# A hybrid decoder layer on one core: the order of the high and low products inside a weight half

## The chip, the core and the metric

The kernel runs on one core of a Trainium2 chip. The metric is the device time of one execution in microseconds. A core has five engines, each with its own instruction queue: TensorE (PE; its weight loads are listed apart as PEld), VectorE (DVE), ScalarE (ACT), GpSimd (POOL) and SyncE (SP), which issues the DMAs here. An engine works off its queue in order and waits on semaphores for what other engines make.

## The reference, cut to what matters

One layer of a decoder trunk over 2048 prompt tokens and 8 x 8 sample tokens, model width 1024, all in fp32: a norm with modulation, the input projection `w_in`, four recurrent mixers (RWKV-7, GLA, gated delta rule, SSD) side by side, the output projection `w_out` with a gated residual, a second norm, and a squared-ReLU MLP with 4096 hidden columns, then a final norm.

```python
h = rmsnorm(x, p['norm1_w']) * (1 + sc1) + sh1
u = jnp.einsum('btd,de->bte', h, p['w_in'])
...
y = jnp.concatenate([y_a, y_b, y_c, y_d], -1) @ p['w_out']
x = x + gt1 * y
h = rmsnorm(x, p['norm2_w']) * (1 + sc2) + sh2
f = jnp.square(jax.nn.relu(h @ p['w_up'])) @ p['w_down']
x = x + gt2 * f
```

The recurrences make the mixers a long chain of small operations; the four projections are the dense work.

## The kernel before

**Three products for one.** TensorE multiplies in fp32r, which holds fewer bits than fp32. So each fp32 operand is split into a high part (its rounding to fp32r) and a low part (the rest), and of the four products three are added up in PSUM: high weight x high activation (line 118), high weight x low activation (line 119), low weight x high activation (line 120). These three lines are nearly all of TensorE's work.

**Weights.** `wload` brings 128 output columns x 1024 inputs of a weight matrix in two halves of 512 (four blocks of 128 inputs each). Per half: a DMA into `wr` (line 100), a cast on ScalarE into the high part `wh` (line 101), and a subtraction `wr - wh` into the low part `wl` (line 103), on VectorE and GpSimd by turns. The rings hold 4 raw, 3 high and 3 low halves, so the cast of a half waits until the high part three halves earlier has had its last reader.

**Products.** `mm3` runs over the four blocks of a half and issues the three products of a block one behind the other. `project` does this for both halves, and in each half for one or two token tiles of 320 to 360 tokens, each with a PSUM bank of its own. A one-tile half is 12 products, a two-tile half 24. The banks are a ring of three (`DPS`).

**Stages.** `stage_A` computes the input projection in four passes over the tokens: one tile, two tiles, two tiles, one tile (`A_PASSES`); ScalarE evacuates each bank into `uo` (line 302), which goes to DRAM. The mixers work on blocks of 256 tokens as soon as their columns are there; their matmuls write `psm`. Beside them go the output projection `F_out` (its transposes are line 338) and the MLP of the first two token blocks, one tile each: `F_up` makes four hidden tiles `f` (ReLU and square on ScalarE, the high part cast there, the low part by VectorE in line 506), and `F_down` multiplies these four with two halves of `w_down` per load, one output tile per half, and adds the result into `acc` on VectorE (line 315). The last 1400 tokens come after the mixers: `quad` computes the up projection by a scheme with seven products of half-size blocks for eight (`forms_w` makes its weight combinations, split in lines 363 and 367), first for one pair of token tiles (from about 2400 us), then for two, and `F_down2` the down projection. All of these call `mm3`.

**Order.** Each lane of the kernel has its priorities: two lanes of mixers go before the dense work, which fills what they leave. The order of every engine's queue is worked out when the kernel is built, by a planner that goes by estimated durations (`schedule_with_timeline_sim=True`, line 2403) and takes what its estimate finds ready; on the chip it is then fixed. So products of mixers stand in the midst of dense groups, and the groups of several PSUM banks can be interleaved.

Of the kernel before, what the change touches and what calls it, by code (L numbers as in the profile page):

```python
# [36 lines left out]
class Dense:  # L37
# [71 lines left out]
        self.tc.add_manual_dep(dma.ins, self.w_dma, mybir.DependencyInfo(mybir.DependencyClass.NoSync, mybir.DependencyReason.SCHED_ONLY),  # L109
                               reason="weights first")  # L110

    def mm3(self, ps, w, ks, first=True, last=True, **kw):

        nc = self.nc
        whi, wlo = w
        for i, (xh, xl) in enumerate(ks):
            lh, ll = whi[:, i * 128 : i * 128 + 128], wlo[:, i * 128 : i * 128 + 128]
            nc.tensor.matmul(ps, lhsT=lh, rhs=xh, start=first and i == 0, stop=False, **kw)  # L118
            nc.tensor.matmul(ps, lhsT=lh, rhs=xl, start=False, stop=False, **kw)  # L119
            nc.tensor.matmul(ps, lhsT=ll, rhs=xh, start=False, stop=last and i == len(ks) - 1, **kw)  # L120

    def project(self, src, xs, tag="d"):

        w = self.wload(src)
        out = [self.psum(tag)[:, :n] for n, _, _ in xs]
        for h in range(2):
            for ps, (n, hi, lo) in zip(out, xs):
                self.mm3(ps, w[h], [(hi[:, k], lo[:, k]) for k in range(4 * h, 4 * h + 4)], h == 0, h == 1)
        return out


# [2275 lines left out]
```

## Time and profile before

| | |
|---|---|
| median of three runs | 3448.45 us (3440.43 to 3454.96) |
| profiled execution | 3452.71 us, span of its instructions 3450.4 us |
| mean granted TensorE clock | 0.953 |
| TensorE busy, products | 3223.8 us (93%), 22902 |
| VectorE / ScalarE / GpSimd busy | 2277.8 / 1474.2 / 1399.2 us |

In the profile's rows PE is a matmul and PEld the load of its weights, which overlaps the matmul before; each product has one of each. `psd<-a,wh` reads: into a PSUM tile `psd`, from the activations `a` and the high weights `wh`; `wl` is the low part, `f` a hidden tile, `sl` a tile of the last stage, `psm` a bank of the mixers. L120 is line 120. A releaser behind `<-` is the instruction whose end let the waiting one go.

### The profile page before, as it was taken

Reading aid. Unit: us, or ns where it says so; the run is one execution under the profiler, and the core shown is the slowest. Engines: PE = TensorE matmul, PEld = TensorE weight load, DVE = VectorE, ACT = ScalarE, POOL = GpSimd, SP = SyncE. Lnnn points to the kernel's source line nnn. Section 1 sums busy time; section 2 is a strip of 40 time slices with the busy share of each in tenths; the row PEclk is TensorE's granted clock in tenths of the full one; section 3 lists DMA queues with packets and bytes.
Section 4 is the critical chain, followed back from the end, with each engine's and each line's share of the span. In section 5 each row is a group of like instructions: output and inputs, shape, how many; then the busy total and the mean of one; then the engine's idle time right before and its main releaser. Section 6 shows DMA issues by size and latency. Waiting matters only on the chain. (4 is left out here: it accounts for less than half of the span.)

```text
span 3450.4 us, 62464 instructions
## 1 busy us (share of the span) xinstructions
PE 3223.8 (93%) x22902; PEld 2947.5 (85%) x22902; DVE 2277.8 (66%) x4728; ACT 1474.2 (43%) x3054; POOL 1399.2 (41%) x1290
## 2 busy tenths in 40 slices
PE   8999999899998989999989988888879999999997
PEld 4779898897997978888868978767879999999997
DVE  3437665866668778889879768768384355445446
ACT  3443433434354454464554454444455566111113
POOL 2333334624335346345446336236275365212112
PEclk9999999999999999999989989978899999999998
DMA  9863344423244565343443333444444455322213
GB/s 301 260 189 114 88 102 134 138 81 108 93 116 124 149 140 137 99 121 103 129 135 121 101 105 96 130 138 152 155 122 125 139 162 173 113 68 99 69 34 122
DMA packets 350394, 438.61 MB, mean 127 GB/s; under 512 B 100626, under 2 KB 228394, under 8 KB 350088
## 3 DMA queue, kind: packets, MB, share of 16 engines
q1 hardware_dynamic: 350088, 434.63, 41.5%
q8 instruction: 180, 2.95, 0.4%
q14 instruction: 126, 1.03, 0.1%
HBM read 346.75 MB, written 87.74 MB: 126 GB/s over the span
## 5 line engine op out<-in xcount | busy, mean ns | idle before, releaser
L103 POOL TENSOR_TENSOR wl<-wr,wh 128x512 fp32r<-128x512 f32 x344 | 477.3, 1389 | 1073.4 <-ACT wh L101 938.6
L120 PE MATMUL psd<-a,wl 128*128 128x360 f32 (+3 forms) x2368 | 798.1, 338 | 25.8 <-DVE wl L103 21.3
L101 ACT CAST wh<-wr 128x512 fp32r<-128x512 f32 x688 | 421.9, 617 | 900.3 <-PE psd L119 418.9
L118 PE MATMUL psd<-a,wh 128*128 128x360 f32 (+3 forms) x2368 | 794.4, 337 | 7.0 <-ACT a L254 3.3
L119 PE MATMUL psd<-a,wh 128*128 128x360 f32 (+3 forms) x2368 | 792.1, 335 | 6.3 <-DVE a L258 2.8
L120 PEld LDWEIGHTS psd<-a,wl 128*128 128x128 f32 x2368 | 456.3, 193 | 67.3 <-DVE wl L103 27.1
L118 PEld LDWEIGHTS psd<-a,wh 128*128 128x128 f32 x2368 | 457.4, 193 | 32.6 <-issue 11.0
L119 PEld LDWEIGHTS psd<-a,wh 128*128 128x128 f32 x2368 | 457.6, 193 | 20.9 <-issue 8.2
L103 DVE TENSOR_TENSOR wl<-wr,wh 128x512 fp32r<-128x512 f32 x344 | 286.5, 833 | 161.6 <-ACT wh L101 145.9
L118 PE MATMUL psd<-sl,wh 128*128 128x350 f32 x992 | 325.8, 329 | 20.9 <-DVE r L484 5.8
L118 PE MATMUL pse<-sl,wh 128*128 128x350 f32 x992 | 325.2, 328 | 7.8 <-DVE s L478 6.0
L120 PE MATMUL pse<-sl,wl 128*128 128x350 f32 x992 | 323.8, 328 | 8.1 <-POOL wl L103 3.8
L119 PE MATMUL psd<-sl,wh 128*128 128x350 f32 x992 | 323.7, 326 | 0.0
L119 PE MATMUL pse<-sl,wh 128*128 128x350 f32 x992 | 322.7, 325 | 0.0
L120 PE MATMUL psd<-sl,wl 128*128 128x350 f32 x992 | 321.6, 326 | 0.3 <-DVE wl L367 0.2
L118 PEld LDWEIGHTS psd<-sl,wh 128*128 128x128 f32 x992 | 189.4, 191 | 23.5 <-issue 6.9
L118 PEld LDWEIGHTS pse<-sl,wh 128*128 128x128 f32 x992 | 189.6, 191 | 9.3 <-ACT wh L363 6.6
L120 PEld LDWEIGHTS pse<-sl,wl 128*128 128x128 f32 x992 | 189.0, 191 | 9.9 <-POOL wl L103 4.0
L118 PE MATMUL psd<-f,wh 128*128 128x352 f32 (+1 forms) x512 | 174.6, 349 | 21.0 <-DVE acc L315 9.1
L120 PEld LDWEIGHTS psd<-sl,wl 128*128 128x128 f32 x992 | 189.5, 191 | 1.2 <-DVE wl L367 0.9
L119 PEld LDWEIGHTS psd<-sl,wh 128*128 128x128 f32 x992 | 190.4, 192 | 0.0
L119 PEld LDWEIGHTS pse<-sl,wh 128*128 128x128 f32 x992 | 189.9, 191 | 0.0
(632 smaller groups left out, 6304.1 us busy)
## 6 DMA issues: line engine op xcount, KB each, us to landing
wr<-w_in SPq DMA_DIRECT2D x256, 256.0 KB
wr<-w_up SPq DMA_DIRECT2D x212, 256.0 KB
wr<-w_down SPq DMA_DIRECT2D x208, 256.0 KB
ada<-ada_w SPq DMA_DIRECT2D x96, 256.0 KB
wr<-w_out SPq DMA_DIRECT2D x96, 256.0 KB
u<-uo SPq DMA_DIRECT2D x128, 180.0 KB
fd<-r SPq DMA_DIRECT2D x128, 175.0 KB
sl<-fd SPq DMA_DIRECT2D x32, 700.0 KB
```

The source lines that it names most:

```text
L101: nc.scalar.copy(hi, raw)
L103: self.lo_eng[self.lo_i % len(self.lo_eng)].tensor_tensor(out=lo, in0=raw, in1=hi.bitcast(F32), op=ALU.subtract)
L118: nc.tensor.matmul(ps, lhsT=lh, rhs=xh, start=first and i == 0, stop=False, **kw)
L119: nc.tensor.matmul(ps, lhsT=lh, rhs=xl, start=False, stop=False, **kw)
L120: nc.tensor.matmul(ps, lhsT=ll, rhs=xh, start=False, stop=last and i == len(ks) - 1, **kw)
```

## The change

`mm3` no longer goes block by block through all three products. It has two parts: first the two products with the high weights for all four blocks, then the product with the low weights for all four. A new argument `half` says whether both parts are issued ("hl") or one of them. `project` issues a first weight half in two goes, the high part of all token tiles and then the low part of all of them; in the second half each token tile has its high and low products together. `F_down`, `F_down2` and `quad` call `mm3` as before and get the new order inside each half. With one tile both halves are then 8 high and 4 low products; with two tiles the first half is 8 + 8 high and 4 + 4 low, the second 8 high, 4 low, 8 high, 4 low.

```diff
-    def mm3(self, ps, w, ks, first=True, last=True, **kw):
+    def mm3(self, ps, w, ks, first=True, last=True, half="hl", **kw):
 
         nc = self.nc
         whi, wlo = w
-        for i, (xh, xl) in enumerate(ks):
-            lh, ll = whi[:, i * 128 : i * 128 + 128], wlo[:, i * 128 : i * 128 + 128]
-            nc.tensor.matmul(ps, lhsT=lh, rhs=xh, start=first and i == 0, stop=False, **kw)
-            nc.tensor.matmul(ps, lhsT=lh, rhs=xl, start=False, stop=False, **kw)
-            nc.tensor.matmul(ps, lhsT=ll, rhs=xh, start=False, stop=last and i == len(ks) - 1, **kw)
+        cols = lambda t, i: t[:, i * 128 : i * 128 + 128]
+        if "h" in half:
+            for i, (xh, xl) in enumerate(ks):
+                nc.tensor.matmul(ps, lhsT=cols(whi, i), rhs=xh, start=first and i == 0, stop=False, **kw)
+                nc.tensor.matmul(ps, lhsT=cols(whi, i), rhs=xl, start=False, stop=False, **kw)
+        if "l" in half:
+            for i, (xh, _) in enumerate(ks):
+                nc.tensor.matmul(ps, lhsT=cols(wlo, i), rhs=xh, start=False, stop=last and i == len(ks) - 1, **kw)
 
     def project(self, src, xs, tag="d"):
 
         w = self.wload(src)
         out = [self.psum(tag)[:, :n] for n, _, _ in xs]
         for h in range(2):
-            for ps, (n, hi, lo) in zip(out, xs):
-                self.mm3(ps, w[h], [(hi[:, k], lo[:, k]) for k in range(4 * h, 4 * h + 4)], h == 0, h == 1)
+            ks = range(4 * h, 4 * h + 4)
+            for half in ("hl",) if h else ("h", "l"):
+                for ps, (n, hi, lo) in zip(out, xs):
+                    self.mm3(ps, w[h], [(hi[:, k], lo[:, k]) for k in ks], h == 0, h == 1, half)
         return out
```

## The prediction

> **What bounds the kernel now.** I read the page's totals first, then the busy time by stage, then TensorE's own list of waits, and at last single places in the timeline.
>
> ```profile
> span 3450.4 us, 62464 instructions
> ...
> PE 3223.8 (93%) x22902; PEld 2947.5 (85%) x22902; DVE 2277.8 (66%) x4728; ACT 1474.2 (43%) x3054; POOL 1399.2 (41%) x1290
> ```
>
> TensorE is busy for 3223.8 of 3450.4 us, so 226.6 us of idle time is what a change of order alone could win directly. The busy time in stretches (columns: stretch, its length, then busy time and count for PE, PEld, DVE, ACT and POOL, granted clock, DMA share, GB/s) shows where that idle time lies:
>
> ```profile
> 195.00:1060.00 865.00, 836.61 (x6572) 751.36 (x6571) 570.56 (x1407) 363.61 (x822) 337.00 (x365) 0.97 0.40 114
> 1060.00:1345.00 285.00, 254.42 (x1947) 227.51 (x1945) 227.76 (x498) 133.46 (x293) 141.16 (x137) 0.93 0.58 143
> 1345.00:2400.00 1055.00, 956.70 (x7404) 863.27 (x7405) 859.28 (x1889) 508.56 (x1059) 472.51 (x440) 0.92 0.39 119
> 2400.00:2600.00 200.00, 162.66 (x914) 156.36 (x913) 128.70 (x170) 95.33 (x193) 105.73 (x80) 0.91 0.43 132
> 2600.00:3400.00 800.00, 798.61 (x4962) 798.06 (x4961) 378.99 (x528) 277.72 (x481) 270.52 (x170) 1.00 0.33 107
> ```
>
> From 2600 to 3400 us TensorE never rests: 800 / 4962 gives 0.161 us from one product to the next, and the order of products cannot help there. From 195 to 1060 us (the two passes with two token tiles) it idles 28 us. From 1060 to 2600 us, where every projection has one token tile and VectorE is over 80% busy up to 2400, it idles 30.6 + 98.3 + 37.3 = 166 us. TensorE's waits (us in total, times, longest) name the part that the change speaks to, and three others that I use below:
>
> ```profile
> PE psd L120 <- DVE wl L103: 30.2, 22, 3.7
> PE psd L120 <- POOL wl L103: 6.0, 6, 2.0
> PE pse L120 <- POOL wl L103: 3.8, 1, 3.8
> PE pse L120 <- DVE wl L367: 2.6, 2, 2.4
> PE pse L120 <- POOL wl L367: 1.7, 1, 1.7
> PE psd L119 <- DVE f L506: 1.6, 2, 1.4
> PE psm L1077 <- DVE dq L1043: 4.5, 1, 4.5
> PE psd L118 <- ACT uo L302: 0.3, 1, 0.3
> ```
>
> The first five rows are the low product (line 120) standing for the low part of a weight half: 32 waits, 44.3 us. In the order of time they begin at 1066 us, all in one-tile stretches, and between 195 and 1060 us there is none. One of them, TensorE and then VectorE at the same moment (start, length, instruction):
>
> ```profile
> 1319.52 0.32 PE L120 MATMUL psd<-a,wl 128*128 128x352 f32 x1
> 1322.12 0.43 PE L120 MATMUL psd<-a,wl 128*128 128x352 f32 x1 [2.28 <-DVE wl L103]
> 1322.39 0.32 PE L118 MATMUL psd<-a,wh 128*128 128x352 f32 x1
> ```
> ```profile
> 1319.61 0.68 DVE L1366 TENSOR_TENSOR t<-t,t 128x512 f32<-128x512 f32 x1
> 1320.21 0.83 DVE L844 COPY t<-gla 128x512 f32<-128x512 f32 x1
> 1320.97 1.10 DVE L103 TENSOR_TENSOR wl<-wr,wh 128x512 fp32r<-128x512 f32 x1
> ```
>
> VectorE is not idle: it works off mixer instructions, and the subtraction that makes the low part stands behind them in its queue. The high part of that half is there, and six more products with it stand in TensorE's queue behind the waiting one.
>
> **The change part by part.** *What stays.* 22902 products and as many weight loads; no DMA, cast, subtraction, PSUM evacuation or buffer is added or removed, so the 3223.8 us of work stay and only idle time and clock can move.
>
> *The low product goes later.* In a one-tile half the first low product is the third of 12 now and the ninth after, 6 x 0.161 = 0.97 us more for the subtraction. At most 32 x 0.97 = 31 us come back. In the timeline 29 of these waits are over 0.3 us, the shortest and the longest being
>
> ```profile
> 1345.28 0.43 PE L120 MATMUL psd<-f,wl 128*128 128x352 f32 x1 [0.34 <-DVE wl L103]
> 2506.40 0.43 PE L120 MATMUL pse<-sl,wl 128*128 128x350 f32 x1 [3.75 <-POOL wl L103]
> ```
>
> 19 of the 29 are longer than 0.97 us and give back 0.97 each (18.4 us), the other 10 all they have (5.5 us): 24 us. Five follow another within 9 us, and there the late VectorE is met again at the next half, so I take 5 off: **-19 us**. Bounds: 0, if each gap only moves to the next wait (VectorE is 81% busy there), and -31.
>
> *The high part comes free earlier.* Its last reader is the eighth product of 12 now in place of the eleventh, 3 x 0.161 = 0.48 us earlier, so ScalarE's next cast can begin earlier. Where I looked (rows above) the subtraction waited for VectorE and not for the cast: I take 0. Bounds 0 and 32 x 0.48 = -15 us.
>
> *The clock.* Idle time costs twice here, because after a stretch with much of it the granted clock halves for one or more stretches of 3.4 us. Four pairs of stretches, before and after such a wait:
>
> ```profile
> 1329.90:1333.30 3.40, 1.27 (x8) 1.28 (x9) 3.40 (x6) 0.50 (x1) 1.52 (x2) 1.00 0.08 16
> 1333.30:1340.10 6.80, 6.80 (x31) 6.80 (x31) 6.19 (x15) 4.40 (x12) 4.09 (x3) 0.50 0.70 206
> 1476.70:1480.10 3.40, 1.74 (x15) 1.26 (x13) 2.91 (x5) 3.40 (x9) 2.19 (x2) 1.00 0.14 38
> 1480.10:1486.90 6.80, 6.80 (x47) 5.85 (x48) 4.03 (x7) 3.15 (x9) 3.31 (x4) 0.50 0.52 159
> 1572.20:1575.60 3.40, 1.34 (x8) 1.34 (x9) 3.40 (x4) 0.71 (x2) 3.40 (x3) 1.00 0.30 98
> 1575.60:1582.40 6.80, 6.80 (x30) 6.19 (x29) 6.80 (x10) 1.80 (x4) 6.70 (x6) 0.50 0.37 116
> 1992.10:1995.50 3.40, 0.80 (x5) 0.81 (x6) 3.37 (x4) 1.11 (x3) 2.00 (x2) 1.00 0.28 64
> 1995.50:2012.60 17.10, 17.10 (x190) 14.57 (x189) 7.44 (x19) 5.40 (x11) 4.84 (x9) 0.50 0.43 119
> ```
>
> Idle time of 2.13, 1.66, 2.06 and 2.60 us in 3.4 stood before them. With 0.97 less the first three fall to 1.2 us and under, below the smallest of the four, the last only to 1.63. I take the first three as saved: 20.4 us at half clock, all busy, are 10 us lost, **-10 us**. Bounds: 0, and (20.4 + 17.1) / 2 = -19 with the fourth.
>
> The Trainium skill ("TensorE: Matmul & The Clock Gate", section "Why this matters for your kernels") asks for no gaps over some 3 us in a row of products, since a whole idle window halves the clock. The trace differs: 1.66 us idle in 3.4 were followed by clock 0.50. By the page's rule none of the three waits above would have cost clock, the term would be 0 and the sum some 10 us smaller.
>
> *What gets worse: the joint between up and down.* F_down's products need four hidden tiles, and the last comes late. The planned order already fills that time by running three PSUM banks up to the last tile:
>
> ```profile
> 2075.51 0.33 PE L118 MATMUL psd<-f,wh 128*128 128x360 f32 x1
> ...
> 2080.91 0.66 PE L118 MATMUL psd<-f,wh 128*128 128x360 f32 x3
> 2082.95 0.43 PE L119 MATMUL psd<-f,wh 128*128 128x360 f32 x1 [1.39 <-DVE f L506]
> ```
>
> Three L118 in a row are three banks arriving at the fourth tile together. Before it they hold 3 x 9 = 27 products; after the change only the high ones of three tiles, 3 x 6 = 18, since the low ones now follow the fourth's high ones. Of the 16 joints 14 go straight over; in six of these the timeline has more than 18 products started before the tile is whole (20, 19, 26, 29, 30, 26), 42 above 18, by 0.161 us **+7 us**. Bounds: 0, where mixer products fill in, and 14 x 9 x 0.161 = +20.
>
> *The two-tile passes.* Both tiles' high products go first, so the second PSUM bank is wanted four products (0.66 us) earlier. The evacuation that frees it takes
>
> ```profile
> L302 ACT COPY uo<-psd x192: 408/452/484, 48.6 to 1309.8; 128x360 f32<-128x360 f32 x128, 128x320 f32<-128x320 f32 x32, 128x352 f32<-128x352 f32 x32
> ```
>
> 0.45 us, 20 products (3.2 us) still lie between, and TensorE waited for it 0.3 us in all: +0.5, bounds 0 and 64 x 0.66 = +42, where each copy came just in time, which that row excludes. The low part gets 14 products more there and nobody waits for it: 0. At the start of each of the two passes the second tile's activations are wanted 0.66 us sooner: +1. The products of two-tile quads after 2600 us: 0, TensorE is full there.
>
> *Sum.* -19 - 10 + 7 + 1.5 = -20.5, say -21 us. The profiled execution took 3452.7 us (span 3450.4 and 2.3 around it), 4.3 above the median of the runs, 3448.45; taken off that median it is **3427 us**. The terms' bounds give 3448.5 - 65 = 3383 and 3448.5 + 22 = 3470.
>
> **Rivals.** *The gaps only move (0.30).* The low part is late because VectorE is, and where TensorE no longer stands at line 120 it stands a little later at the next instruction that VectorE owes it. For it: VectorE's 859 of 1055 us. Against: a queue with 19% of slack can catch up within the microsecond given. If a third of the -19 is kept, the stretches stay idle enough for half clock (the page's rule above also gives a clock term of 0, by another road), and the joint costs its 7: 3448.5 - 6 + 7 - 4 (a little of the earlier cast) = 3445.
>
> *The joint decides (0.09), slower.* If in all 14 joints the last tile comes after 18 products and no mixer product is ready, each costs 9 x 0.161 = 1.45 us and, like 1.66 us above, a half-clock stretch of 6.8 us, 3.4 lost: 14 x 4.85 = 68 less 29, 3448.5 + 39 = 3487. For it: the three-bank pattern. Against: 1.6 us of waits for f today. It turns the sign when more than 6 joints (29 / 4.85) pay in full.
>
> *The order is planned anew (0.10), slower.* The order on each engine is worked out when the kernel is built, from estimated durations (line 2403), and longer runs of dense products change what fits between mixer products. One place now costs as follows, when a mixer's serial chain ran with no dense product put beside it:
>
> ```profile
> 1763.40:1797.50 34.10, 18.77 (x115) 15.00 (x114) 26.86 (x48) 19.82 (x43) 15.80 (x15) 0.50 0.34 95
> ```
>
> 15.3 us idle and half of 18.8 lost: 25 us. Two such places more make 3427 + 50 = 3477. One more ends at 3452, no change; the sign turns at one. Against: dense work is the filler and its amount is the same. A luckier plan is as possible and lies in the range's lower end.
>
> **How the numbers follow.** The sum as worked out, with its gain: 0.50, own range 3395 to 3431. With 0.30, 0.09 and 0.10 as above, and 0.01 left over, the predicted time is 3427. What a measurement here tells from no change is about 0.5%, 17 us. Faster by more than that: 0.50; within: 0.31; slower: 0.19. Low end 3390, near the terms' lower bound; high end 3466, which takes in the moving gaps and one unlucky place and leaves out about 0.13 above and 0.06 below.
>
> **What will show it.** Right: the rows of line-120 waits, 44.3 us now, fall under 25; the granted clock, 0.93 and 0.92 in the two stretches from 1060 to 2400, rises by 0.01 or more; PE count stays 22902. Wrong on the joint: waits for f (L506) well over 1.6 us. Gaps moved: the low product's waits fall but waits for acc L315, wh L101 and mixer tiles rise by as much. Replanned: a new stretch like 1763 to 1797. The prediction fails most simply if products with the same rate no longer follow at 0.161 us after 2600 us.

## Result and profile after

| | before | after |
|---|---|---|
| median of the runs beside each other | 3452.03 us (6 runs, 3440.43 to 3454.96) | 3428.98 us (6 runs, 3426.07 to 3431.08) |
| ratio, 95% interval | | 0.9939 [0.9926, 0.9951] |
| span of the profiled execution | 3450.4 us | 3428.5 us |

The changed kernel is 0.6% faster, 21 to 23 us; the prediction was 3427 us and 21 us less. The total came out; the terms behind it only in part, and that the others cancel is luck (the sum is in the part on why). The page's totals of the changed kernel:

```profile
span 3428.5 us, 62450 instructions
...
PE 3196.0 (93%) x22902; PEld 2934.5 (86%) x22902; DVE 2253.6 (66%) x4728; ACT 1475.3 (43%) x3054; POOL 1397.0 (41%) x1290
```

TensorE's idle time did not fall: 3428.5 - 3196.0 = 232.5 us, 226.6 before. All of the gain is in its *busy* time, with the same 22902 products at the same distance. Two things sit in busy time that are no work. Products at half clock count as busy all along. And a product's record lasts 0.32 us where the next one starts after 0.161, so the first 0.16 us of any wait lies under the record of the product before: the wait shown as 2.28 us at 1322.12 was 2.60 from start to start, 2.44 lost. In what follows I therefore add up starts to starts, less 0.161 us (0.147 for 320 columns, 0.165 for 360), and give the rest to half clock or to what the next product waited for.

The stretches of the changed kernel, with the columns as before:

```profile
195.00:1060.00 865.00, 839.95 (x6609) 753.91 (x6608) 583.56 (x1412) 370.06 (x831) 337.74 (x367) 0.97 0.40 115
1060.00:1345.00 285.00, 251.54 (x1924) 226.96 (x1923) 222.32 (x498) 129.75 (x284) 136.20 (x134) 0.90 0.56 141
1345.00:2400.00 1055.00, 941.89 (x7415) 856.57 (x7414) 875.61 (x1900) 513.26 (x1066) 480.45 (x445) 0.92 0.39 119
2400.00:2600.00 200.00, 170.35 (x1008) 167.06 (x1009) 126.18 (x170) 104.58 (x212) 110.76 (x85) 0.93 0.46 145
2600.00:3400.00 800.00, 795.74 (x4934) 794.96 (x4933) 355.49 (x548) 271.15 (x475) 265.56 (x167) 1.00 0.33 110
```

TensorE's waits; the low product is line 123 now, the high ones lines 119 and 120, `f` is made in lines 510 and 511:

```profile
PE psd L119 <- ACT sl L402: 16.6, 1, 16.6
...
PE psd L120 <- DVE f L511: 9.7, 5, 4.8
...
PE psm L1439 <- DVE KB L1416: 8.2, 5, 4.7
...
PE psd L123 <- DVE wl L103: 6.1, 6, 1.9
...
PE pse L123 <- DVE wl L372: 5.4, 2, 4.8
...
PE pse L123 <- POOL wl L103: 2.0, 1, 2.0
...
PE psd L123 <- POOL wl L103: 1.2, 2, 0.7
```

The waits of low products are down from 44.3 us to 16 us (these four rows and two small ones). New on the list are one wait of 16.6 us for `sl`, the activations of the last stage, and more waits for `f` and for mixer tiles.

**Where the time went, by three stretches.** I cut both executions at 1060 us, at the last product of F_down, and at the 1000th product of the last stage.

| stretch | before | after |
|---|---|---|
| 1060 us to the last F_down product | 1340.4 us | 1299.6 us |
| to the 1000th product of the last stage | 223.8 us | 242.5 us |
| to the end | 826.3 us | 826.4 us |

The middle of the kernel gained 41 us and the step into the last stage gave 19 of them back. Within the first stretch (starts to starts, as above):

| 1060 us to the last F_down product, us | before | after |
|---|---|---|
| low product waits for `wl` | 42.0 | 7.6 |
| half clock on dense products | 35.9 | 27.0 |
| PSUM bank not yet free (`acc`, `xp`) | 16.9 | 4.4 |
| waits for `f` | 2.1 | 12.6 |
| mixer products waiting | 55.6 | 79.0 |
| dense products' own time | 757.8 | 748.9 |

Not all of the stretch is in these rows. They add up to 910.3 and 879.5 us; the rest, 430.1 and 420.1 us, mostly the mixers' own products, is 10 us smaller and is not taken apart here. The last row is work that was already done by 1060 us: 9 of the 41 us were won in the passes before, where no low product had waited.

**The step that gives back.** The end of F_down and what follows, first in the kernel before, then in the changed one:

```profile
2400.21 0.32 PE L120 MATMUL psd<-f,wl 128*128 128x360 f32 x1
2400.57 0.40 PE L118 MATMUL psd<-sl,wh 128*128 128x350 f32 x1
```
```profile
2358.90 0.82 PE L123 MATMUL psd<-f,wl 128*128 128x360 f32 x4
2360.50 0.40 PE L119 MATMUL psd<-sl,wh 128*128 128x350 f32 x1 [0.77 <-DVE acc L320]
...
2361.06 0.32 PE L120 MATMUL psd<-sl,wh 128*128 128x350 f32 x1
2377.97 0.66 PE L119 MATMUL psd<-sl,wh 128*128 128x350 f32 x1 [16.59 <-ACT sl L402]
```

Before, the last stage found its activations made and went on at once. After, F_down ends 41 us sooner and TensorE stands before the second block for 16.59 us, because ScalarE and VectorE make these activations no sooner. When each kernel casts the first of them and when it ends F_down shows in these groups (durations, then first and last start), before and then after:

```profile
L397 ACT ACTIVATE sl<-d,mod x24: 573/588/596, 2348.7 to 2572.2; 128x350 fp32r<-128x350 f32 x24
L120 PE MATMUL psd<-f,wl x512: 317/324/667, 1345.3 to 2400.2; 128*128 128x352 f32 x86, 128*128 128x360 f32 x85
```
```profile
L402 ACT ACTIVATE sl<-d,mod x24: 576/587/592, 2355.5 to 2554.9; 128x350 fp32r<-128x350 f32 x24
L123 PE MATMUL psd<-f,wl x512: 318/326/502, 1335.5 to 2359.4; 128*128 128x352 f32 x86, 128*128 128x360 f32 x85
```

I call the start of the first cast of `sl` X and the end of F_down F. Before: X 2349, F 2400. After: X 2356, F 2360.

### The profile page after: what moved, and what is told of

Its sections match the earlier page's. It is cut to its first block, busy times and chain, and to the rows that moved or that the text cites. A ratio compares the mean times of both kernels' runs of the same rounds, so it can differ in the third digit from the quotient of the medians.

```text
span 3428.5 us, 62450 instructions
## 1 busy us (share of the span) xinstructions
PE 3196.0 (93%) x22902; PEld 2934.5 (86%) x22902; DVE 2253.6 (66%) x4728; ACT 1475.3 (43%) x3054; POOL 1397.0 (41%) x1290
## 5 line engine op out<-in xcount | busy, mean ns | idle before, releaser
L123 PE MATMUL psd<-a,wl 128*128 128x360 f32 (+3 forms) x2368 | 504.5, 333 | 6.8 <-DVE wl L103 5.2
L123 PEld LDWEIGHTS psd<-a,wl 128*128 128x128 f32 x2368 | 400.7, 191 | 37.7 <-issue 21.7
L103 DVE TENSOR_TENSOR wl<-wr,wh 128x512 fp32r<-128x512 f32 x344 | 273.3, 795 | 157.8 <-ACT wh L101 122.0
L119 PE MATMUL psd<-sl,wh 128*128 128x350 f32 x992 | 323.7, 328 | 31.5 <-ACT sl L402 16.6
L119 PEld LDWEIGHTS psd<-sl,wh 128*128 128x128 f32 x992 | 190.2, 192 | 33.7 <-ACT sl L402 16.9
L123 PE MATMUL pse<-sl,wl 128*128 128x350 f32 x992 | 200.8, 326 | 7.9 <-DVE wl L372 5.4
L123 PE MATMUL psd<-sl,wl 128*128 128x350 f32 x992 | 200.2, 326 | 0.9 <-DVE wl L372 0.9
L120 PE MATMUL psd<-f,wh 128*128 128x352 f32 (+1 forms) x512 | 171.4, 338 | 9.9 <-DVE f L511 9.7
L877 DVE SCALAR_TENSOR_TENSOR t<-u,cw,t 128x256 f32<-128x256 f32 x288 | 178.5, 659 | 0.9
L119 PE MATMUL psd<-f,wh 128*128 128x352 f32 (+1 forms) x512 | 168.1, 340 | 11.0 <-DVE d L324 4.8
```

Source lines behind the costliest of these rows:

```text
L103: self.lo_eng[self.lo_i % len(self.lo_eng)].tensor_tensor(out=lo, in0=raw, in1=hi.bitcast(F32), op=ALU.subtract)
L119: nc.tensor.matmul(ps, lhsT=cols(whi, i), rhs=xh, start=first and i == 0, stop=False, **kw)
L120: nc.tensor.matmul(ps, lhsT=cols(whi, i), rhs=xl, start=False, stop=False, **kw)
L123: nc.tensor.matmul(ps, lhsT=cols(wlo, i), rhs=xh, start=False, stop=last and i == len(ks) - 1, **kw)
L877: nc.vector.scalar_tensor_tensor(out=y[:, q], in0=uv[:, q, i : i + n], scalar=w(i), in1=y[:, q], op0=ALU.mult, op1=ALU.add)
```

## The experiments

Ratios are to the kernel before on the same chip, with 95% intervals. F and X are of the profiled execution, S is the start of the product that follows the 1000th of the last stage (called the 1000th product below), and wl is the sum of the low products' waits between 1060 us and F (or S for the two kernels marked *).

| kernel | ratio | F | X | S | S - F | S - X | wl |
|---|---|---|---|---|---|---|---|
| before | 1 | 2400.5 | 2348.7 | 2624.2 | 224 | 275 | 42.0 |
| after | 0.9939 [0.9926, 0.9951] | 2359.7 | 2355.5 | 2602.1 | 242 | 247 | 7.6 |
| e1 order alone | 0.9968 [0.9953, 0.9983] | 2375.7 | 2369.1 | 2620.8 | 245 | 252 | 13.2 |
| e2 two-tile split alone | 1.0006 [0.9993, 1.0019] | 2413.0 | 2353.3 | 2631.5 | 218 | 278 | 44.5 |
| e3 low products first | 0.9978 [0.9965, 0.9990] | 2403.6 | 2313.2 | 2619.0 | 215 | 306 | 69.5 |
| e4 F_down in the old order | 0.9956 [0.9941, 0.9972] | 2378.0 | 2369.7 | 2616.0 | 238 | 246 | 27.5 |
| e5 before, plan 1 | 1.0034 [1.0006, 1.0061] | 2416.3 | 2364.1 | 2640.5 | 224 | 276 | 44.7 |
| e6 after, plan 1 | 0.9972 [0.9961, 0.9982] | 2363.5 | 2357.0 | 2609.3 | 246 | 252 | 9.0 |
| e7 before, plan 2 | 0.9991 [0.9981, 1.0000] | 2386.2 | 2351.7 | 2621.4 | 235 | 270 | 36.5 |
| e8 after, plan 2 | 0.9968 [0.9949, 0.9987] | 2359.4 | 2363.5 | 2601.5 | 242 | 238 | 17.2 |
| e9 before, lighter * | 0.9921 [0.9904, 0.9939] | | 2354.6 | 2603.5 | | 249 | 51.5 |
| e10 after, lighter * | 0.9896 [0.9878, 0.9914] | | 2341.0 | 2587.1 | | 246 | 17.7 |
| e11 before, plan 3 | 1.0013 [1.0002, 1.0025] | 2404.7 | 2362.0 | 2632.4 | 228 | 270 | 40.3 |
| e12 after, plan 3 | 1.0016 [1.0003, 1.0029] | 2411.7 | 2315.3 | 2629.0 | 217 | 314 | 3.6 |

From S to the end every one of them takes 821 to 827 us, so S decides. F, X and S are of one execution each, and that one is not always near the median of its kernel: e8's is 9.8 us below it, e4's 9.3 and e1's 6.8 us above. Differences of under 10 us between two kernels are therefore not read from these columns; differences between F, X and S of one kernel are of the same execution.

**e1, the order inside a half alone.**

```diff
-            for half in ("hl",) if h else ("h", "l"):
+            for half in ("hl",):
```

> Change: the new order inside a half (8 high products, then 4 low) everywhere, without the split over two token tiles in a first half. Theory A (the low part is late in one-tile stretches, and the low product now comes 0.97 us later): all of the gain is here; low-product waits on wl under 25 us as in the changed kernel (44.3 before), time 0.993 to 0.996 of before. Theory B (the gain is a lucky new plan of the queues, whatever moved): the time can lie anywhere within 0.99 to 1.01 of before, although the wl waits fall.

Measured 0.9968: half of the gain, just outside theory A's range, with the waits where A put them (13.2 us). F is 25 us sooner than before, but X is 20 us later, and the 1000th product of the last stage comes 252 us after X.

**e2, the two-tile split alone.** As the changed kernel, but every half other than the first of a two-tile projection goes through its blocks in the old order.

```diff
+        if half == "hl":
+            for i, (xh, xl) in enumerate(ks):
+                nc.tensor.matmul(ps, lhsT=cols(whi, i), rhs=xh, start=first and i == 0, stop=False, **kw)
+                nc.tensor.matmul(ps, lhsT=cols(whi, i), rhs=xl, start=False, stop=False, **kw)
+                nc.tensor.matmul(ps, lhsT=cols(wlo, i), rhs=xh, start=False, stop=last and i == len(ks) - 1, **kw)
+            return
...
-            for half in ("hl",) if h else ("h", "l"):
+            for half in ("hl",) if h or len(xs) == 1 else ("h", "l"):
```

> Change: only a two-tile first half is split (8 + 8 high, then 4 + 4 low); all other halves keep the old order, block by block. Theory A: no low product waited in the two-tile passes, so no gain: wl waits stay at 35 to 50 us, time within 0.3% of before (0.997 to 1.003). Theory B: the plan behind these passes is another one, so the time moves by up to 0.7% one way or the other though nothing was waiting there.

Measured 1.0006: nothing, as A said. By itself the split does not move the time. Together e1 and e2 leave half of the gain unassigned: 0.9968 x 1.0006 = 0.9974 against 0.9939. Whether the two parts help each other or the plan of the whole change is a lucky one, these two runs do not tell; the neutral edits below move a kernel by as much.

**e3, the contrary: the low products of a half first.**

```diff
+        for i, (xh, _) in enumerate(ks):
+            nc.tensor.matmul(ps, lhsT=cols(wlo, i), rhs=xh, start=first and i == 0, stop=False, **kw)
+        for i, (xh, xl) in enumerate(ks):
+            nc.tensor.matmul(ps, lhsT=cols(whi, i), rhs=xh, start=False, stop=False, **kw)
+            nc.tensor.matmul(ps, lhsT=cols(whi, i), rhs=xl, start=False, stop=last and i == len(ks) - 1, **kw)
```

> Change: the contrary: inside a half the 4 low products go first, then the 8 high ones. The first low product is then the first of a half, 0.32 us sooner than before, and 1.29 us sooner than in the changed kernel. Theory A: wl waits grow from 44 us to 55 to 80 us and the time to 1.003 to 1.010 of before. Theory B: no tie between the waits on wl and the time; 0.99 to 1.01.

The waits on `wl` grew as expected, to 80 us in TensorE's list, of which the three largest rows are

```profile
PE psd L118 <- DVE wl L103: 50.7, 29, 7.9
...
PE psd L118 <- POOL wl L103: 14.3, 10, 2.8
...
PE pse L118 <- DVE wl L368: 6.4, 2, 4.9
```

and the kernel was not slower but 0.2% faster. Theory A as I had put it, that the sum of these waits is the time, has fallen. Between 1060 us and F the 27 us more on `wl` stand against 10 less on `acc`, 6 on `xp`, 9 in mixer products and 6 on `wh`: a VectorE that is late is met somewhere, and the row that names it is only the first place. X is 35 us earlier than before, F 3 us later, S 5 us sooner.

**e4, F_down alone back in the old order.** `F_down` calls `mm3` with the block order of e2, chosen here by a value of its own.

```diff
-                    self.mm3(ps, w[ci], [(fh[:, o : o + n], fl[:, o : o + n]) for fh, fl in f])
+                    self.mm3(ps, w[ci], [(fh[:, o : o + n], fl[:, o : o + n]) for fh, fl in f], half="blocks")
```

> Change: the changed kernel with the old order, block by block, in F_down alone. Joint theory (the new order lets fewer products run before the last hidden tile, waits on f 9.7 us after against 1.6 before): waits on f fall back to under 4 us, waits on wl in front of F_down products return by some 8 to 12 us, so the time stays within 0.3% of the changed kernel (0.991 to 0.997 of before). Theory B: 0.99 to 1.01, with waits on f falling all the same.

Measured 0.9956. Waits for `f` fell from 12.6 to 7.7 us between 1060 us and F, not below 4 as expected, and waits on `wl` rose by 20, of which some 12 stand before F_down's products. The time is within the range, slightly above the changed kernel. Taking part of the wait at the joint of F_up and F_down away brought nothing.

**e5 to e8, e11, e12: the same kernels under other plans.** Each pair has one edit that leaves work and instructions as they are and makes the planner lay the queues out anew: the turn of VectorE and GpSimd in `modulate` (plan 1) or in `wload` (plan 3) begins with the other engine, or the next pass's norms are asked for two output tiles earlier (plan 2). Plan 3 is the least neutral of the three: the engine that makes the low part of a weight half changes for every half (in the traces the first is made by VectorE before and by GpSimd here), and the wait under test is for that part.

```diff
-        self.uid = self.lo_i = self.mod_i = self.y_i = 0
+        self.uid = self.lo_i = self.y_i = 0
+        self.mod_i = 1
```
```diff
-        self.uid = self.lo_i = self.mod_i = self.y_i = 0
+        self.uid = self.mod_i = self.y_i = 0
+        self.lo_i = 1
```
```diff
-            if i + 1 < len(A_PASSES) and j in (16, 22)[: len(A_PASSES[i + 1])]:
-                self.norm_A(*A_PASSES[i + 1][j == 22])
+            if i + 1 < len(A_PASSES) and j in (14, 20)[: len(A_PASSES[i + 1])]:
+                self.norm_A(*A_PASSES[i + 1][j == 20])
```

> Change: the kernel before with one neutral edit: the turn by which modulate shares its low parts between VectorE and GpSimd begins with the other engine (mod_i = 1). Same work, same number of instructions; the queues are planned anew. Theory B (luck of the plan): 0.993 to 1.007 of before. Theory A (what counts is when the low product stands): 0.998 to 1.002, wl waits 35 to 50 us.

> Change: the changed kernel with the same neutral edit (mod_i = 1). Theory A: the changed kernel's gain stays against its partner with the same edit, 0.993 to 0.996 of it, and wl waits are under 25 us. Theory B: the gain over its partner lies anywhere from -0.7% to +0.7%, though the wl waits are under 25 us.

> Change: the kernel before with another neutral edit: the norm of the next pass is asked for two output tiles earlier (j = 14 and 20 in place of 16 and 22). Theory B: 0.993 to 1.007 of before. Theory A: 0.998 to 1.002.

> Change: the changed kernel with the norms two output tiles earlier. Theory A: 0.993 to 0.996 of its partner with the same edit. Theory B: from -0.7% to +0.7% of it, though the wl waits are under 25 us.

> Change: the kernel before with a third neutral edit: the turn by which low parts of weights go to VectorE and GpSimd begins with the other engine (lo_i = 1). A measure of the plan's own spread: 0.996 to 1.004 of before.

> Change: the changed kernel with lo_i = 1. The two pairs so far gave 0.992 and 0.997 of their partner, the kernels themselves 0.994. Theory A: 0.992 to 0.997 of its partner again, its last F_down product 25 to 50 us earlier, about half of it given back until the 1000th product of the last stage. Theory B (luck of the plan alone): 1.00 or more is as likely as less.

The neutral edits moved the kernel before by -0.1 to +0.3%, and the changed one by +0.3, +0.3 and +0.8%. The changed kernel against its partner (quotient of the two ratios, half-widths added in squares): 0.9939 as given, 0.994 [0.991, 0.997] in plan 1, 0.998 [0.996, 1.000] in plan 2, 1.000 [0.998, 1.002] in plan 3. It was never slower; in two plans of four it gained over 0.5%. The waits on `wl` fall by 19 to 37 us in all four, and half clock on dense products by 6 to 11 us. Theory B allows that, since it says only that the time can go either way whatever the waits do; four pairs of which none got slower, 0.4% faster on average, speak against it and do not exclude it. Theory A does not explain why plan 3 gained nothing. In plan 3 the waits are gone as nowhere else:

```profile
PE psd L206 <- DVE ssum L241: 21.8, 2, 11.0
...
PE psd L214 <- POOL rsc L222: 11.3, 2, 6.4
...
PE psd L124 <- DVE wl L104: 1.5, 3, 0.5
PE pse L124 <- DVE wl L373: 1.1, 1, 1.1
```

but TensorE stands for the norms of a token block (`ssum`, `rsc`), 33 us in these two rows against 16 in its partner (of which one wait of 10 to 11 us, at the very start, is in both), and the two ends lie so:

```profile
L403 ACT ACTIVATE sl<-d,mod x24: 572/587/593, 2315.3 to 2581.5; 128x350 fp32r<-128x350 f32 x24
L124 PE MATMUL psd<-f,wl x512: 318/326/641, 1382.9 to 2411.4; 128*128 128x352 f32 x86, 128*128 128x360 f32 x85
```

X came 47 us sooner than in its partner and F 7 us later. The mixers' last product came 44 us sooner too (2283 against 2328). So the time set free went to the mixers and the activations, while the dense work, which ended last already, came no sooner; what of this is the price of the 17 us more for the norms, no run separates.

**Two floors.** In the table the kernels fall into two groups. Where F is much later than X (before, e2, e3, e5, e11, e12), S is 215 to 228 us after F, while S - X runs from 270 to 314. Where X is about as late as F or later (after, e1, e4, e6, e9, e10), S is 246 to 252 us after X, while S - F runs from 238 to 246 (e9 and e10 have no such F). So S is near the later of F + 221 and X + 248, two numbers taken from these runs themselves. With 826 to the end, before: 2400.5 + 221 + 826 = 3447.5 (span 3450.4); after: 2355.5 + 248 + 826 = 3429.5 (3428.5). Two kernels do not fit: e7, between the groups, is 14 us above F + 221, and e8 is 10 us below X + 248. Why stays open.

**e9 and e10: less dense work.** This is to tell two floors from one path. Both kernels leave out 192 products of `F_down`, so their output is no longer the layer's. The edit in both:

```diff
-                K.F_down(bi, f, acc, cc)
+                if not (final and cc >= 6):
+                    K.F_down(bi, f, acc, cc)
```

> Leaves out: F_down of the last two of eight hidden groups in the second small token block (192 products, 192 x 0.165 = 32 us of dense work) in the kernel before. Theory C (two floors: the last stage begins when the dense filler is done AND when the mixers are done; the 1000th product of the last stage comes 218 us after the last F_down product or 276 us after the last mixer product, whichever is later; before: 2400 + 224 = 2624 against 2316 + 276 = 2592): the kernel before is bound by its dense work and gains 25 to 32 us, 0.990 to 0.993 of before. Theory D (one additive path: each us of dense work counts, in both kernels): the same here, -32 us, 0.991.

> Leaves out: the same 192 products in the changed kernel. Theory C: the changed kernel already waits for the mixers (2326 + 276 = 2602, its 1000th product at 2602), so 32 us less dense work gain only 0 to 10 us: 0.991 to 0.994 of before, as e9 or within 0.3% of it, with the last F_down product some 30 us earlier and the last stage's waits for its activations (sl) up by 20 to 30 us. Theory D: another 32 us, 0.984 to 0.986 of before.

The kernel before gained 0.8% (27 us) and its S came to 249 us after X: it ran into the other floor. It now waits for the activations of the last stage, which the full kernel before did not:

```profile
PE psd L118 <- ACT sl L397: 14.7, 2, 11.0
...
PE psd L119 <- DVE sl L398: 12.7, 4, 4.4
```

The changed kernel gained 0.9896 / 0.9939 = 0.996 [0.994, 0.998], some 15 us and not 32; theory D's 0.984 to 0.986 lies outside the interval, theory C's 0.991 to 0.994 above most of it. So one additive path is excluded, and theory C just touches the measured interval. What it gained is X, 14 us sooner, and S is again 246 us after X; why X came sooner is not shown. TensorE had run out of work ahead of X: from 2320 to 2341 us it is busy for 5.9 of 21 us. It waits for its activations in two places, and for a norm:

```profile
PE pst L213 <- POOL rsc L221: 14.7, 3, 10.5
...
PE psd L119 <- ACT sl L402: 10.9, 1, 10.9
...
PE psd L120 <- DVE sl L403: 9.6, 4, 5.0
```

The waits for `sl` were to rise by 20 to 30 us and rose by some 2 (16.6 + 1.6 us in the changed kernel, 10.9 + 9.6 here). I had tied the second floor to the mixers' last product (276 us after it in three kernels); here S comes 266 us after it, in e9 273, and X fits more of them. Whether the mixers' end, the norm of the output projection or VectorE's load holds X back, no run here separates.

## Why the prediction was right or wrong

**The low product goes later (-19, bounds 0 and -31).** The mechanism was right: the waits fell from 44.3 to 16 us on the list, and from 42.0 to 7.6 between 1060 us and F. The size was mis-set: 28 us on the list is near the far bound, 34 us from start to start beyond it. What I left out is the 0.16 us of each wait that lies under the record before it, some 5 us for 32 waits. Whether the earlier cast, which I had taken at 0, made up the rest, no run shows.

**The clock (-10).** Half clock on dense products fell by 8.9 us, from 35.9 to 27.0, in 24 stretches of 212 us in all before and 19 of 195 us after. So the size came out, but not the way to it. First, the places: at nearly the times of two of the three stretches that I took as saved, the changed kernel has half clock again. Second, the rule: I had taken idle time as the cause, with 1.66 us in 3.4 as the least that does it. The traces have half clock behind stretches in which TensorE was hardly idle, one in each kernel (the two rows of before and the last two of after, below, whose first two rows are the places named first):

```profile
1094.40:1097.80 3.40, 3.09 (x26) 2.80 (x25) 1.75 (x6) 3.40 (x9) 2.91 (x4) 1.00 0.78 97
1097.80:1101.20 3.40, 3.40 (x14) 3.40 (x13) 2.41 (x6) 0.93 (x2) 0.77 (x3) 0.50 0.79 211
```
```profile
1333.50:1340.30 6.80, 5.28 (x18) 4.89 (x19) 6.39 (x19) 3.18 (x6) 3.24 (x3) 0.50 0.23 72
1575.80:1586.00 10.20, 7.50 (x33) 7.27 (x33) 10.20 (x16) 1.87 (x3) 10.10 (x10) 0.50 0.16 54
1831.80:1835.20 3.40, 3.33 (x26) 3.07 (x27) 3.40 (x7) 0.43 (x2) 3.04 (x3) 1.00 0.43 132
1835.20:1838.60 3.40, 3.40 (x14) 3.40 (x13) 3.37 (x8) 0.62 (x1) 2.49 (x5) 0.50 0.42 129
```

Idle for 0.31 and 0.07 us in 3.4, and clock 0.50 behind them. Most of the products in these two stretches are the mixers', 16 and 8 of them only two columns wide; what in these stretches brings the half clock, no run here tells. So the agreement of -10 and -8.9 is in good part luck.

The sign that I named for the term failed too: the granted clock went from 0.93 to 0.90 and stayed at 0.92. It is a mean over time, and half clock in stretches where TensorE stands anyway lowers it at little cost; in the wait for `sl` it was so:

```profile
2360.00:2378.00 18.00, 0.91 (x5) 0.65 (x5) 18.00 (x28) 7.33 (x15) 10.42 (x9) 0.62 0.24 67
```

Idle for 17 of 18 us, clock 0.62; this much the Trainium skill's section that I cited ("TensorE: Matmul & The Clock Gate", "Why this matters for your kernels") describes too. By its rule alone, with nothing below some 3 us counted, the 8.9 us would not have been there: behind single waits of 3 us or more the dense products lost some 3 us at half clock in either kernel.

**The joint between up and down (+7, bounds 0 and +20).** Waits for `f` rose by 10.5 us between 1060 us and F, 9.7 in one row of the list where 1.6 was the sum. The sign and nearly the size came out in this pair, but the term is no steady price of the new order: the kernel before waits 6.4 and 10.7 us in this row under plans 1 and 2, the changed one 2.9 and 10.0. As a rival that decides it fell: e4 takes part of the wait away and gains nothing.

**The two-tile passes (+1.5, the rest 0).** e2 shows no effect on the time: 1.0006 [0.9993, 1.0019]. Yet the changed kernel was ahead by 9 us of dense work at 1060 us. Its third pass, the second with two tiles, has its last evacuation (line 302) done at 1025.5 us, 1035.6 before, and in the four other pairs, e9 and e10 among them, the changed kernel is 3 to 24 us ahead of its partner there. I had +1.5 for these passes. Where the lead comes from is open: in e2 that evacuation is 18 us later than before.

**What I did not foresee, and the luck in the sum.** Two terms that I had at nothing cost time: mixer products wait 23.4 us more between 1060 us and F, and the last stage gives back 18.7 us, since its activations come no sooner. Against them stand gains that I had not: the waits on `wl` gave 15 us more than the 19, those for PSUM banks 12.5 us, the passes up to 1060 us 9 us, and 10 us came in the rest of the stretch that the rows do not name. Added up in the order `wl`, half clock, `f`, up to 1060 us, banks, rest, mixers, last stage: -34.4 - 8.9 + 10.5 - 8.9 - 12.5 - 10.0 + 23.4 + 18.7 = -22.1 us. That 42 us of unforeseen cost met about as much unforeseen gain is luck. I wrote that TensorE might stand "a little later at the next instruction that VectorE owes it" and never asked when the next stage's own inputs are ready. The row for X stood in the trace of before: 2349 against F 2400. With the 248 us that the later runs give for S - X, no more than 2624 - 2597 = 27 us could be won at that end, whatever F gained, as long as X stays (it moved from 2313 to 2370 us over these kernels).

**The rivals.** "The gaps only move" is half of the truth: in idle time they moved altogether (226.6 to 232.5 us), in plan 3 in time as well. "Planned anew" is real with a spread of -0.1 to +0.8% by neutral edits, as large as the gain itself, but in none of four plans was the changed kernel slower than its partner. The chance of 0.50 for faster by over 0.5% against 0.31 for no change is about what the four plans show: two and two.

## What to carry to other kernels

Before you count a wait as gain, look up when the next stage's inputs are ready: the time between the end of the stage that you speed up and that moment is the most that you can win, as long as that moment stays where it is. A row of waits names the first place where a late engine is met, not its price; moving the reader later frees time that a planner may hand to other work, and what bounds the end decides what it is worth. Where queues are planned by estimates, test a reordering under a few neutral edits on both sides before believing a half per cent.

## What the runs showed of the hardware

Idle TensorE time and busy TensorE time can both mislead: 22902 products were 27.8 us less busy with the same distance between them, 0.161 us, because half clock and the first 0.16 us of each wait count as busy. Half clock does not need much idle time: it followed 3.4 us with 1.66, 0.31 and even 0.07 us idle. And low products first, with 80 us of waits on `wl` against 44, cost nothing.
